# Eleven weight blocks multiplied in full precision, and a new order of gate work at the head of each chunk

## The chip, the cores and the metric

The kernel runs on one core of one Trainium2 chip. The metric is the device time of one execution in microseconds (us). A core has five engines that run side by side, each through its own list of instructions in order: TensorE (PE, matrix products; its weight loads are shown apart as PEld), VectorE (DVE), ScalarE (ACT), GpSimd (POOL) and SyncE (SP), which here only starts transfers. They wait for one another through semaphores.

## What is computed

One encoder block on 512 tokens of 1024 numbers. A first half (a convolution and a recurrence, projections in and out) makes `x1`; the second half, where this change lies, is a PEER layer: of 16384 one-neuron experts each token picks 16 per head, for 8 heads.

```
q = (h @ w_q);  sc = q . sub_keys                # two 128-wide score rows per head
top_s, top_i = top_k(sc, 16)                     # per half
best_s, best_pos = top_k(all 16 x 16 sums, 16)   # the 16 experts of a head
g = softmax(best_s)
act = gelu(expert_u[idx] . h)
y = sum_k g * act * expert_v[idx]
x = x + g2 * y;  out = rmsnorm(x)
```

## The kernel before, in words

The tokens stand in four tiles of 128. For the tokens from 192 on (320 of them, `NU`) the kernel doesn't gather experts: it multiplies every block of 128 experts with all of them and masks the result by gates. For tile 0 and the first 64 tokens of tile 1 it gathers rows of `expert_u` and `expert_v` by index: one gather on POOL and one product with a sum on DVE (a *dot step*, `scr`, L823) for each.

**Precision.** A product of two float32 operands is made of three products in the reduced format `fp32r`. ACT rounds a weight block to `whi` (`high`, L75), DVE subtracts it from the block to get the rest, `wlo` (`low`, L80), and PE multiplies `whi` by the rounded activations, `whi` by their rest and `wlo` by the rounded ones (`mm3`, L89, L90, L91): 8 slices of 128 rows times 3, so 24 products of 128x320 a block.

**Phases.** A first half; the queries and scores; then the *activation phase*: a loop over `k`, one *chunk* for each of 124 weight blocks of `expert_u` (`CE`), with PE results evicted by ACT through GELU (`u_evict`, L888, two PSUM buffers). Then the *output phase*, 128 blocks of `expert_v` (`acc`, L1070) with the last four of `expert_u` among them, and the sums for the gathered rows (`ys`, L839); last the final norm.

**The order in the activation phase** is written by a planner when the program is built. It keeps three accounts of nanoseconds by fixed costs, `pe`, `dve` and `ac`, and fills each chunk with items of DVE work until the `dve` account reaches the `pe` account. An engine then simply follows its list. The generators are:

- `s`, the searches: the top 16 of the scores and of the candidate sums of a tile (`topk_tile`). It ends in one-hot comparisons for which ACT spreads a key over 2048 numbers (`oh`, L604) and takes the exponent for the softmax (L607). The exponent and GELU each load their table first.
- `r`, the top 16 of the scores for the remaining tiles. When it has ended, the gates may begin.
- `g`, the gates. One item of the wide kind prepares 8 tokens: DVE makes one-hots (`oh`, L662) and their high halves times the gate (`igh`, L667); ACT makes the low halves, one instruction a token (`gates_low`, L678, also `igh`). The item also issues, on PE, the 16 products (L693) of the group prepared by the `g` item before it, and on ACT the copies (`stg`, L702) of the one before that, which are stored to memory in pieces of 512 KB (`Gd`). A narrow kind (L652, L655, L690) serves 4 tokens, with float32 products; there are 16 such steps.
- `d`, the dot steps.

In a chunk `k` the kernel starts the load of block `k+5`, issues `low` for block `k+2`, the 24 products and the eviction of the chunk before, up to four low halves; then come the items, and at the end `high` for block `k+3`. The three loads for blocks 2 to 4 stand ahead of the loop. `HEAD` lets DVE's account begin 6000 ns low, so that the first chunks take more items.

Of the kernel before, what the change touches and what calls it, by code (L numbers as in the profile page):

```python
# [8 lines left out]
F32 = mybir.dt.float32  # L9
FR = mybir.dt.float32r  # L10
# [3 lines left out]
AF = mybir.ActivationFunctionType  # L14
# [3 lines left out]
T = 512  # L18
D = 1024
KB = 8  # L20
# [14 lines left out]
def block_kernel(ctx, tc, xT, small, w_ada1, w_ada, b_ada, w_in, w_r, w_i, w_out, w_q, keys, uT, u, v, final_g, out):  # L35
    nc = tc.nc
# [4 lines left out]
    wring = ctx.enter_context(tc.tile_pool(name="wring", bufs=2))  # L41
# [26 lines left out]
    def load_w(src):  # L68
        raw = wring.tile([128, KB, 128], F32, name="wraw", bufs=WR)
        nc.sync.dma_start(raw, src)  # L70
        return raw
# [15 lines left out]
    def mm3(ps, hi, lo, xh, xl, ks, first, last):  # L87
        for k in ks:
            nc.tensor.matmul(ps, hi[:, k, :], xh(k), start=first and k == ks[0], stop=False)  # L89
            nc.tensor.matmul(ps, hi[:, k, :], xl(k), start=False, stop=False)  # L90
            nc.tensor.matmul(ps, lo[:, k, :], xh(k), start=False, stop=last and k == ks[-1])  # L91
# [12 lines left out]
    adac = const.tile([128, 48], F32, name="adac")  # L104
# [114 lines left out]
    def modulate(t1, k, A, B, hh, hl, full=None):  # L219
        f = sq_pool.tile([128, T], F32, name="mfull")  # L220
        nc.vector.tensor_scalar(f, t1, A[:, k:k + 1], B[:, k:k + 1], op0=OP.mult, op1=OP.add)
        nc.scalar.activation(hh[:, k, :], t1, AF.Identity, scale=A[:, k:k + 1], bias=B[:, k:k + 1])
        nc.vector.tensor_sub(hl[:, k, :], f, hh[:, k, :].bitcast(F32))
        if full is not None:
            full(k, f)
# [15 lines left out]
    z_, tn, e_, w_, w2, ac = (l4[:, i, :] for i in range(6))  # L241
# [166 lines left out]
    for m in range(KB):  # L408
# [3 lines left out]
        ps = psZ.tile([128, T], F32, name="ps_z", bufs=3)  # L412
# [31 lines left out]
    A2 = const.tile([128, KB], F32, name="A2")  # L444
    nc.vector.scalar_tensor_tensor(A2, adac[:, 32:40], 1.0, sm("n2g"), op0=OP.add, op1=OP.mult)
    h2n = persist.tile([128, D], F32, name="h2n")
    sel = ctx.enter_context(tc.tile_pool(name="sel", bufs=1, side="right"))
    h2b = sel.tile([128, D], F32, name="h2b")

    def full2(k, f):  # L450
        if k % 4 == 0:
# [10 lines left out]
    for k in range(KB):  # L462
        t1 = sq_pool.tile([128, T], F32, name="mt1")
        nc.vector.tensor_mul(t1, xs[:, k, :], psr2)
        modulate(t1, k, A2, adac[:, 24:32], h2h, h2l, full2)


    ep = ExitStack()
    ring = ctx.enter_context(tc.tile_pool(name="ring", bufs=1, side="right"))
    scp = ep.enter_context(tc.tile_pool(name="scp", bufs=1, side="right"))  # L470
    top = scp.tile([128, NT, 8, 2, 16], F32, name="top")
    ti = scp.tile([128, NT, 8, 2, 16], U32, name="ti")
# [25 lines left out]
    qsp = {}  # L498
    early = chain(*(stage1([h], range(NT)) for h in range(HQ)))

    ND = T - 128
    NU = ND - XB
    hd = lambda k: h2h[:, k, T - NU:]
    ld = lambda k: h2l[:, k, T - NU:]

    for h in range(8):
# [8 lines left out]
        ps = psZ.tile([128, T], F32, name="ps_z", bufs=3)  # L515
# [50 lines left out]
    def topk_tile(t):  # L566
# [17 lines left out]
        g = g_s.rearrange("p (h k) -> p h k", h=8) if t == 0 else topk.tile([128, 8, 16], F32, name="g")  # L584
# [12 lines left out]
        for w in range(2):  # L597
            oh = topk.tile(shp, F16, name="oh")
            if w == 1:
                pf = topk.tile([128, 8, 16], F16, name="pf")  # L600
                nc.vector.tensor_copy(pf, msk)
            yield None
            key, ref, cmp, src = ((pf, st16, OP.is_ge, dif), (pf, io16, OP.is_equal, tif[:, :, 1, :]))[w]
            nc.scalar.activation(oh, key[:, :, :, None].to_broadcast(shp), AF.Copy)  # L604
            ac[0] += 1930
            if w == 0:
                nc.scalar.activation(g, g, AF.Exp)  # L607
            yield None
            nc.vector.tensor_tensor(oh, oh, ref[:, None, None, :].to_broadcast(shp), op=cmp)
            nc.vector.tensor_tensor(oh, oh, src[:, :, None, :].to_broadcast(shp), op=OP.mult)  # L610
            yield 2300
            for n in (8, 4, 2):
                nc.vector.tensor_add(oh[:, :, :, 0:n], oh[:, :, :, 0:n], oh[:, :, :, n:2 * n])
            nc.vector.tensor_add(ij[:, w], oh[:, :, :, 0], oh[:, :, :, 1])
            yield 1400
# [57 lines left out]
    def gates_low(n):  # L673
        for _ in range(n):
            if lows:
                of, ig, gl, t0 = lows[0]
                k = next(low_k)
                nc.scalar.activation(ig[:, 1, k // 2, :, k % 2], of[:, k // 2, 0, :, k % 2], AF.Copy,  # L678
                                     scale=gl[:, t0 + k:t0 + k + 1])
                if k == 7:  # L680
                    lows.pop(0)
# [165 lines left out]
    jobs = [("u", c) for c in range(CE)]  # L847
# [4 lines left out]
    wraw, whi, wlo = {1: qraw[9]}, {}, {}  # L852
# [3 lines left out]
    def w_load(k):  # L856
        if k < len(jobs):
            kind, i = jobs[k]
            wraw[k] = load_w(uT[i] if kind == "u" else
                             v[vorder[i] * 128:(vorder[i] + 1) * 128, :].rearrange("p (k e) -> p k e", k=KB))  # L860

    def w_high(k):
        if k < len(jobs):
            whi[k] = high(wraw[k])

    def w_low(k):
        if k < len(jobs):
            wlo[k] = low(wraw.pop(k), whi[k])

    def weights(k):  # L870
# [3 lines left out]
    act = {0: act0}  # L874
# [15 lines left out]
    def u_chunk(k, pool):  # L890
        c = jobs[k][1]
        if c:
            ps = pool.tile([128, NU], F32, name="ps_act", bufs=2)
            mm3(ps, whi.pop(k), wlo.pop(k), hd, ld, range(KB), True, True)
            u_evict()
            unread.append((c, ps))
        q = c // 2 - RB // 2 + 2
        if c % 2 == 0 and 0 <= q < v0 // 2:
            spill(q)
        pe[0] += 3530  # L900
        dve[0] += 1140
        ac[0] += 1400

    gbuf, g16, gdone = {}, {}, set()
    coef = {}
# [71 lines left out]
    def turn(k):  # L977

        awake = [g for g in "gsrd" if g in gens and asleep[g] <= k]
        if "d" in awake and (given["d"] >= DR * (k + 1 - first[0]) or k >= CE - QU or xd > k % 2):  # L980
            awake.remove("d")
        if gopen and "g" in gens:
            gt = 96 * (k + 1 - gopen[0]) / (KD - KG - gopen[0])
            if "g" in awake and given["g"] < gt and ac[0] < pe[0] + AD:
                return "g"
            if "s" in awake and (given["g"] < gt or given["s"] < NS * (k - gopen[0]) / (SE * (KD - gopen[0]))):
                return "s"
        elif "s" in awake:
            return "s"
        elif "r" in awake and ("d" not in awake or given["d"] >= DS * (k - first[0])):  # L990
            return "r"
        for g in "dsg" if ac[0] < pe[0] + AD else "ds":
            if g in awake:
                return g
# [8 lines left out]
    for k in range(CE):  # L1003
        weights(k)
        u_chunk(k, psE)
        gates_low(4)
        cur[0] = k
        if sready and not first:
            first.append(k + 4)
            asleep["d"] = k + 4  # L1010
            for m in range(GB_E - 1):
                gath(u, usteps[m][0], usteps[m][3], m)
        ac[0] = max(ac[0], pe[0] - LEAD)
        dve[0] = max(dve[0], RHO * pe[0] - LEAD - (HEAD if k < 9 else 0))
        xd = 0
        while dve[0] < RHO * pe[0] or k == KD:
            g = turn(k)
            if k == KD:
                g = next((g for g in "sg" if g in gens), None)
                if "s" not in gens and len(bdone) < XB:  # L1020
                    g = "d"
            if g is None or (g == "d" and "g" not in gens and xd >= XD):
                break
            n = next(gens[g], 0)
            if n == 0:
                assert g != "d"
                late_k[g] = k
                del gens[g]
                continue
            if n is None:  # L1030
                asleep[g] = k + 1
                continue
            dve[0] += n
            xd += g == "d"
            if gopen or g == "d":
                given[g] += {"g": 0, "d": 1}.get(g, n)
        w_high(k + 3)
        if k == KD:
            ep.close()
            vp = ctx.enter_context(tc.tile_pool(name="vp", bufs=2, reuse_waits="tile"))  # L1040
            gp = ctx.enter_context(tc.tile_pool(name="gp", bufs=1, reuse_waits="tile"))
            late[:] = [gp, taken[0] + 10]
            gt8 = vp.tile([128, 2, NG, 8, 16], F32, name="gt", bufs=1)
        m = k - CE + XE
        if 0 <= m < XE:
            for n in [0] if m < 2 else range(5) if m == XE - 1 else [8]:
                v_gates(n)
        if m >= XE - 2:
            (v_gated, v_rest)[m - XE + 2](0)
# [105 lines left out]
XB = 64  # L1155
GS = 32768.0
GPE = 460
SE = 0.65
AD = 500
LEAD = 3500  # L1160
RHO = 1.0
VE = 1
KG = 4
HEAD = 6000
NS = 56000
DS = 1.0
XD = 2
# [60 lines left out]
```

## Time and profile before

| | |
|---|---|
| median of 3 runs | 1394.5 us (1393.42 to 1398.49) |
| profiled execution, whole | 1394.83 us |
| its span, first to last instruction | 1393.0 us |
| mean granted TensorE clock | 0.985 |
| activation phase, chunks 1 to 123 | 294 to 817 us of the span |
| output phase and end | 817 to 1393 us |

The span is what the trace covers; 1.8 us of the profiled execution lie around it. In the views that follow, a line such as `L80` is a line of the kernel before, "out<-in" names what an instruction writes and reads, and a bracket at the end of a row of the timeline is the idle time of that engine just before the instruction, with what ended it.

### The profile page before, as it was taken

The page shows a single profiled execution, that of the slowest core. Times are in us where ns is not written, and L with a number is a line of the kernel's source. Part 1 is how long each engine was busy: PE and PEld are TensorE (multiplying, and loading weights), DVE is VectorE, ACT ScalarE, POOL GpSimd, SP SyncE. Part 2 cuts the span into 40 slices and gives each one's busy share as a digit, 9 for nine tenths or more (in the row PEclk, how much of TensorE's full clock was granted, in tenths as well). Part 3 has the DMA queues.
Part 4 walks back from the last instruction along what each step waited for, and adds up shares of the span by engine and source line. Part 5 has one row for each costly group of instructions (what it writes and reads, how often), then busy time and mean ns, then how long its engine had stood idle before and what let it go on. Part 6 is the DMA issues. An engine that isn't in the chain of part 4 may idle for free.

```text
span 1393.0 us, 21402 instructions
## 1 busy us (share of the span) xinstructions
PE 1321.6 (95%) x7571; PEld 1135.5 (82%) x7571; DVE 1235.1 (89%) x2313; ACT 706.6 (51%) x1202; POOL 532.7 (38%) x334
## 2 busy tenths in 40 slices
PE   5999999989999999999999999899999999999995
PEld 2676787789989899998999998787878787878884
DVE  6878756999999999999999748799999889898998
ACT  4666644434567797787744443333243334333442
POOL 0000000000233244445445305576766566676760
PEclk9999999999999999999999999999999999999998
DMA  8776322224688899999999988999999999999994
GB/s 349 264 271 219 115 91 84 69 92 133 230 287 292 289 369 394 331 377 361 417 381 395 411 274 278 391 392 416 413 415 413 398 404 413 411 415 412 418 380 171
DMA packets 146928, 440.06 MB, mean 316 GB/s; under 512 B 14722, under 2 KB 42370, under 8 KB 144772
## 3 DMA queue, kind: packets, MB, share of 16 engines
q1 hardware_dynamic: 99812, 267.75, 52.2%
q0 software_dynamic: 46720, 169.89, 31.0%
q8 instruction: 59, 0.97, 0.3%
q10 hardware_dynamic: 288, 1.05, 0.2%
q14 instruction: 49, 0.40, 0.1%
HBM read 393.54 MB, written 45.09 MB: 315 GB/s over the span
## 4 chain that ended last, share of the span: by engine, by line
PE 47%; DVE 22%; DMA 13%; issue 12%; ACT 5%; DVEq 0%; SPq 0%; POOL 0%; ACTq 0%
DMA wraw<-in_v_dram 10%; PE acc L1070 8%; PE ps_act L89 6%; PE ps_act L91 6%; PE ps_act L90 6%; PE ps_z L89 5%; PE ps_z L90 5%; PE ps_z L91 5%; DVE wlo L80 4%; DVE scr L823 4%; DVE ys L839 3%; DMA Gd<-stg 2%; DVE cl L965 2%; DVE cf L954 2%; PE ps_gt L693 2%
## 5 line engine op out<-in xcount | busy, mean ns | idle before, releaser
L75 ACT ACTIVATE whi<-wraw 128x1024 fp32r<-128x1024 f32 x292 | 308.7, 1057 | 361.2 <-DMA wraw<-in_v_dram 204.6
L80 DVE TENSOR_TENSOR wlo<-wraw,whi 128x1024 fp32r<-128x1024 f32 x292 | 356.2, 1220 | 91.5 <-ACT whi L75 90.3
L89 PE MATMUL ps_act<-h,whi 128*128 128x320 f32 x1016 | 321.2, 316 | 5.4 <-ACT act L888 5.2
L91 PE MATMUL ps_act<-h,wlo 128*128 128x320 f32 x1016 | 316.2, 311 | 4.0 <-DVE wlo L80 4.0
L90 PE MATMUL ps_act<-h,whi 128*128 128x320 f32 x1016 | 315.9, 311 | 0.0
L802 POOL DMA_INDIRECT rows<-in_u_dram,idx_s x128 | 200.0, 1562 | 187.1 <-DVE scr L823 159.9
L802 POOL DMA_INDIRECT rows<-in_v_dram,idx_s x128 | 218.6, 1708 | 112.2 <-DVE ys L839 89.1
L1070 PE MATMUL acc<-whi,cl 128*128 128x512 f32 x750 | 233.5, 393 | 9.0 <-DVE cl L965 8.9
L1070 PE MATMUL acc<-whi,ch 128*128 128x512 f32 x750 | 232.8, 392 | 6.6 <-ACT ch L958 6.0
L1070 PE MATMUL acc<-wlo,ch 128*128 128x512 f32 x750 | 232.0, 390 | 0.0
L802 POOL DMA_INDIRECT rows<-in_u_dram,idx_b x64 | 108.9, 1702 | 264.4 <-DVE scr L823 171.6
L89 PEld LDWEIGHTS ps_act<-h,whi 128*128 128x128 f32 x1016 | 192.9, 190 | 8.0 <-ACT act L888 7.1
L91 PEld LDWEIGHTS ps_act<-h,wlo 128*128 128x128 f32 x1016 | 192.6, 190 | 4.3 <-DVE wlo L80 4.3
L90 PEld LDWEIGHTS ps_act<-h,whi 128*128 128x128 f32 x1016 | 192.8, 190 | 0.2
L1070 PEld LDWEIGHTS acc<-whi,cl 128*128 128x128 f32 x750 | 140.2, 188 | 43.5 <-DVE cl L965 15.1
L1070 PEld LDWEIGHTS acc<-whi,ch 128*128 128x128 f32 x750 | 140.7, 189 | 37.9 <-ACT ch L958 8.3
L1070 PEld LDWEIGHTS acc<-wlo,ch 128*128 128x128 f32 x750 | 141.4, 188 | 29.8
L839 DVE SCALAR_TENSOR_TENSOR ys<-rows,acts,ys 128x1024 f32<-128x1024 f32 x127 | 162.6, 1281 | 1.7
L823 DVE SCALAR_TENSOR_TENSOR scr<-rows,h2n 128x1024 f16<-128x1024 f32 x128 | 156.2, 1220 | 2.7 <-DMA rows<-in_u_dram,idx_s 1.0
L678 ACT ACTIVATE igh<-oh,gl 128x128 f16<-128x128 f16 x320 | 104.0, 431 | 47.3 <-DVE oh L662 47.1
L433 POOL DMA_DIRECT2D x1d<-xn x8 | 4.5, 570 | 258.8 <-ACT xn L432 258.8
L888 ACT ACTIVATE act<-ps_act 128x320 f32<-128x320 f32 x127 | 54.9, 433 | 90.6 <-PE ps_act L91 90.4
(277 smaller groups left out, 1750.6 us busy)
## 6 DMA issues: line engine op xcount, KB each, us to landing
wraw<-in_uT_dram SPq DMA_DIRECT2D x128, 512.0 KB, 6.4
wraw<-in_v_dram SPq DMA_DIRECT2D x128, 512.0 KB, 10.2
Gd<-stg SPq DMA_DIRECT2D x46, 512.0 KB, 8.9
wada<-in_w_ada_dram SPq DMA_DIRECT2D x16, 1024.0 KB, 5.3
Ad<-act SPq DMA_DIRECT2D x48, 320.0 KB, 7.0
act<-Ad SPq DMA_DIRECT2D x48, 320.0 KB, 12.6
h<-Gd SPq DMA_DIRECT2D x12, 1024.0 KB, 17.3
wraw<-in_w_in_dram SPq DMA_DIRECT2D x20, 512.0 KB, 6.0
```

The costliest lines, as they stand in the source:

```text
L75: nc.scalar.activation(hi, raw, AF.Copy)
L80: nc.vector.tensor_sub(lo, raw, hi.bitcast(F32))
L89: nc.tensor.matmul(ps, hi[:, k, :], xh(k), start=first and k == ks[0], stop=False)
L90: nc.tensor.matmul(ps, hi[:, k, :], xl(k), start=False, stop=False)
L91: nc.tensor.matmul(ps, lo[:, k, :], xh(k), start=False, stop=last and k == ks[-1])
L678: nc.scalar.activation(ig[:, 1, k // 2, :, k % 2], of[:, k // 2, 0, :, k % 2], AF.Copy, scale=gl[:, t0 + k:t0 + k + 1])
L693: nc.tensor.matmul(pg[:, k, :], oh[:, a, 1, :, b], ig[:, w, a, :, b], start=w == 0, stop=w == 1)
L802: nc.gpsimd.indirect_dma_start(out=r[:, :], out_offset=None, in_=table, in_offset=bass.IndirectOffsetOnAxis(ap=idxs[:, k:k + 1], axis=0))
L823: nc.vector.scalar_tensor_tensor(scr, rows.pop(n), 1.0, hn, op0=OP.mult, op1=OP.mult, accum_out=dst[:, k:k + 1])
L839: nc.vector.scalar_tensor_tensor(ys, rows.pop(k), acts[:, k:k + 1], ys, op0=OP.mult, op1=OP.add)
L888: nc.scalar.activation(act[c // 2][:, c % 2], ps, AF.Gelu)
L1070: nc.tensor.matmul(accs[b][e], st[:, bs], mv[:, e * 512:(e + 1) * 512], start=first, stop=last)
```

## The change

1. **Blocks 1 to 11 of `expert_u` unsplit.** For `k < FN = 12` there is neither `high` nor `low`. PE multiplies the raw float32 block by a float32 copy of the activations, `h2f`: 8 products in place of 24. The copy is made when the activations are: one more ACT instruction of 128x320 for each of 8 slices, in four buffers that the ring `act` otherwise uses later. Blocks 5 to 11 are loaded into the buffers of `whi` and `wlo`, which are free then.
2. **Accounts.** Such a chunk counts 4400 ns on `pe` (`FPE`), nothing for the subtraction on `dve` and 450 on `ac`. `HEAD` is 0.
3. **One `g` item a chunk.** After a `g` item the gates sleep until the next chunk. Dot steps may run ahead a little by the number of chunks since the gates ended (`DX`).
4. **ACT at the head of a chunk.** `high(k+3)` stands right behind the eviction, then up to 8 low halves instead of 4.
5. In the search of tile 1 one more pause of a chunk ahead of the first one-hots.

```
+    h2f = [ring.tile([128, 2, NU], F32, name="act", bufs=RB // 2) for _ in range(KB // 2)]
...
         modulate(t1, k, A2, adac[:, 24:32], h2h, h2l, full2)
+        nc.scalar.activation(h2f[k // 2][:, k % 2], t1[:, T - NU:], AF.Identity, scale=A2[:, k:k + 1],
+                             bias=adac[:, 24 + k:25 + k])
...
             yield None
+            if t == 1 and w == 0:
+                yield None
...
     def w_load(k):
+            if 5 <= k < FN:
+                raw = wring.tile([128, KB, 128], FR, name=("wlo", "whi")[k % 2], bufs=WB).bitcast(F32)
+                nc.sync.dma_start(raw, uT[i])
+                wraw[k] = raw
+                return
     def w_high(k):
-        if k < len(jobs):
+        if FN <= k < len(jobs):
     def w_low(k):
-        if k < len(jobs):
+        if FN <= k < len(jobs):
...
     def u_chunk(k, pool):
-            mm3(ps, whi.pop(k), wlo.pop(k), hd, ld, range(KB), True, True)
+            if k < FN:
+                raw = wraw.pop(k)
+                for j in range(KB):
+                    nc.tensor.matmul(ps, raw[:, j, :], h2f[j // 2][:, j % 2], start=j == 0, stop=j == KB - 1)
+            else:
+                mm3(ps, whi.pop(k), wlo.pop(k), hd, ld, range(KB), True, True)
...
-        pe[0] += 3530
-        dve[0] += 1140
-        ac[0] += 1400
+        pe[0] += FPE if c and k < FN else 3530
+        dve[0] += 0 if c and k < FN - 2 else 1140
+        ac[0] += 450 if c and k < FN - 3 else 1400
...
-        if "d" in awake and (given["d"] >= DR * (k + 1 - first[0]) or k >= CE - QU or xd > k % 2):
+        if "d" in awake and (given["d"] >= DR * (k + 1 - first[0]) + DX * max(k - late_k.get("g", k), 0) or k >= CE - QU or xd > k % 2):
...
         weights(k)
         u_chunk(k, psE)
-        gates_low(4)
+        w_high(k + 3)
+        gates_low(8)
...
+            if g == "g" and k < KD:
+                asleep[g] = k + 1
...
-        w_high(k + 3)
...
+FN = 12
+DX = 0.3
+FPE = 4400
-HEAD = 6000
+HEAD = 0
```

On PE the first chunks read as follows. Before, the start of chunk 1 (`h_83` are the activations in the reduced format):

```order
L89 MATMUL ps_act<-h_83,whi 128x320
L90 MATMUL ps_act<-h_83,whi 128x320
L91 MATMUL ps_act<-h_83,wlo 128x320
L89 MATMUL ps_act<-h_83,whi 128x320
L90 MATMUL ps_act<-h_83,whi 128x320
L91 MATMUL ps_act<-h_83,wlo 128x320
```

Now, chunks 1 to 9 (32 products for chunks 1 to 4, whose blocks lie in `wraw`, then 8 a chunk; the `act` that is read is `h2f`):

```order
L907 MATMUL ps_act<-act,wraw 128x320 x32
L907 MATMUL ps_act<-act,whi 128x320 x8
L907 MATMUL ps_act<-act,wlo 128x320 x8
L907 MATMUL ps_act<-act,whi 128x320 x8
L907 MATMUL ps_act<-act,wlo 128x320 x8
L907 MATMUL ps_act<-act,whi 128x320 x8
```

No product of chunks 1 to 11 waits for ACT or DVE any more, apart from the eviction of its buffer.

On DVE, the chunk that holds the sixth and seventh wide group (chunk 28), before:

```order
L80 TENSOR_TENSOR wlo<-wraw,whi 128x1024
L662 TENSOR_TENSOR oh_4095<-io_2603,selT 128x2048
L667 TENSOR_TENSOR igh<-oh_4095,gh 128x1024
L823 SCALAR_TENSOR_TENSOR scr,act_b<-rows,h2b 128x1024
L662 TENSOR_TENSOR oh_4133<-io_2603,selT 128x2048
L667 TENSOR_TENSOR igh<-oh_4133,gh 128x1024
L80 TENSOR_TENSOR wlo<-wraw,whi 128x1024
```

Now, the seventh and eighth wide group (chunks 26 and 27):

```order
L80 TENSOR_TENSOR wlo<-wraw,whi 128x1024
L667 TENSOR_TENSOR oh_3869<-io_2615,selT 128x2048
L672 TENSOR_TENSOR igh<-oh_3869,gh 128x1024
L828 SCALAR_TENSOR_TENSOR scr,act_b<-rows,h2b 128x1024
L80 TENSOR_TENSOR wlo<-wraw,whi 128x1024
L828 SCALAR_TENSOR_TENSOR scr,act_b<-rows,h2b 128x1024
L604 CAST pf<-msk 128x128
L667 TENSOR_TENSOR oh_3948<-io_2615,selT 128x2048
L672 TENSOR_TENSOR igh<-oh_3948,gh 128x1024
```

Two groups no longer stand in one chunk. Before, the second `g` item of such a chunk had PE multiply the group that the first one had only just prepared; chunks 28, 39 and 82 held two wide groups, and chunks 94, 98, 102, 106 and 110 two narrow ones.

On ACT, the same chunk 28 before, with the eviction of chunk 28 at its end (`high` is the last piece of a chunk):

```order
L888 ACTIVATE act<-ps_act 128x320
L678 ACTIVATE igh<-oh_3968,gl 128x128 x4
L702 ACTIVATE stg<-ps_gt 128x128x4 x2
L678 ACTIVATE igh<-oh_4095,gl 128x128 x8
L702 ACTIVATE stg<-ps_gt 128x128x4 x2
L75 ACTIVATE whi<-wraw 128x1024
L888 ACTIVATE act<-ps_act 128x320
```

And now, in chunks 26 to 28:

```order
L898 ACTIVATE act<-ps_act 128x320
L75 ACTIVATE whi<-wraw 128x1024
L707 ACTIVATE stg<-ps_gt 128x128x4 x2
L898 ACTIVATE act<-ps_act 128x320
L75 ACTIVATE whi<-wraw 128x1024
L683 ACTIVATE igh<-oh_3869,gl 128x128 x8
L707 ACTIVATE stg<-ps_gt 128x128x4 x2
L898 ACTIVATE act<-ps_act 128x320
```

The rounding has moved from behind the low halves and copies to ahead of them, and all 8 low halves of a group stand in the chunk after the one in which DVE prepared it.

More of the change, by code (lines that the diff above doesn't have):

```diff
@@ L448, in block_kernel @@
     h2b = sel.tile([128, D], F32, name="h2b")
+    ring = ctx.enter_context(tc.tile_pool(name="ring", bufs=1, side="right"))
+    ND = T - 128
+    NU = ND - XB
+    h2f = [ring.tile([128, 2, NU], F32, name="act", bufs=RB // 2) for _ in range(KB // 2)]
     def full2(k, f):
@@ L465, in block_kernel @@
         modulate(t1, k, A2, adac[:, 24:32], h2h, h2l, full2)
+        nc.scalar.activation(h2f[k // 2][:, k % 2], t1[:, T - NU:], AF.Identity, scale=A2[:, k:k + 1],
+                             bias=adac[:, 24 + k:25 + k])
     ep = ExitStack()
-    ring = ctx.enter_context(tc.tile_pool(name="ring", bufs=1, side="right"))
     scp = ep.enter_context(tc.tile_pool(name="scp", bufs=1, side="right"))
@@ L499, in block_kernel @@
     early = chain(*(stage1([h], range(NT)) for h in range(HQ)))
-    ND = T - 128
-    NU = ND - XB
     hd = lambda k: h2h[:, k, T - NU:]
```

## The prediction

> **What bounds the kernel now.** I read the page's busy shares first, then the stages, then who waited for whom on PE and DVE, and last the rows around PE's long waits.
>
> ```profile
> PE 1321.6 (95%) x7571; PEld 1135.5 (82%) x7571; DVE 1235.1 (89%) x2313; ACT 706.6 (51%) x1202; POOL 532.7 (38%) x334
> core 0: us, PE busy (x) PEld busy (x) DVE busy (x) ACT busy (x) POOL busy (x), PEclk, DMA share, GB/s
> 294.00:342.50 48.50, 42.52 (x272) 41.40 (x268) 47.72 (x225) 23.35 (x30) 0.00 (x0) 0.93 0.37 114
> 342.50:412.00 69.50, 65.87 (x489) 64.43 (x489) 69.04 (x261) 38.31 (x85) 20.80 (x13) 1.00 0.70 235
> 412.00:465.00 53.00, 48.30 (x349) 46.80 (x350) 47.93 (x84) 37.28 (x75) 17.96 (x11) 0.97 0.90 316
> 465.00:640.00 175.00, 172.77 (x1387) 169.54 (x1385) 172.62 (x339) 146.59 (x326) 71.59 (x41) 1.00 0.94 347
> 640.00:690.00 50.00, 47.35 (x368) 46.50 (x369) 48.70 (x63) 39.48 (x96) 27.78 (x19) 0.93 1.02 410
> 690.00:750.00 60.00, 56.73 (x409) 55.91 (x408) 54.47 (x106) 25.81 (x45) 28.53 (x20) 1.00 1.02 386
> 750.00:817.00 67.00, 66.81 (x469) 66.55 (x467) 49.97 (x79) 29.33 (x45) 21.65 (x16) 1.00 1.03 388
> 817.00:1360.00 543.00, 527.65 (x2325) 432.67 (x2326) 490.99 (x536) 201.36 (x259) 339.23 (x203) 0.99 1.00 392
> ```
>
> In the activation phase (294 to 817) both PE and DVE are nearly full up to 690; from 750 DVE has room. So the phase is worth what PE loses in it, as long as DVE can follow. PE loses most in 294 to 342, 412 to 465 and 640 to 690, which are also the stages where the granted clock (PEclk) is below 1. These are its waits from 294 to 817, and DVE's from 285 to 700 (us in total, times, longest):
>
> ```profile
> PE ps_gt L693 <- DVE igh L667: 6.5, 2, 3.3
> PE ps_act L89 <- ACT act L888: 5.2, 5, 1.6
> PE ps_act L91 <- DVE wlo L80: 4.0, 1, 4.0
> PE ps_gt L690 <- DVE oh L655: 2.3, 1, 2.3
> PE ps_gt L693 <- ACT igh L678: 1.9, 2, 1.3
> PE ps_gt L690 <- ACT stg L702: 0.9, 1, 0.9
> DVE wlo L80 <- ACT whi L75: 8.1, 6, 3.0
> DVE st L554 <- PE ps_g L525: 1.7, 1, 1.7
> ```
>
> DVE waits 9.8 us in 415: it is the second bound, right behind PE.
>
> **The change part by part.**
>
> *Float32 products.* Now, 24 products of a block take the distance of these two rows, 3.52 us; eleven blocks 38.7. The two rows of float32 products in the trace follow.
>
> ```profile
> 294.60 0.31 PE L89 MATMUL ps_act<-h,whi 128*128 128x320 f32 x1
> 298.12 0.31 PE L89 MATMUL ps_act<-h,whi 128*128 128x320 f32 x1
> 48.81 1.04 PE L135 MATMUL ps_row<-wada,cs 128*1 128x512 f32 x8
> L135 PE MATMUL ps_row<-wada,cs 128*1 128x512 f32 x128 | 16.6, 591 | 0.0
> 750.66 1.78 PE ps_gt L690 x16
> L690 PEld LDWEIGHTS ps_gt<-oh x128: 186/192/192, 697.2 to 774.2; 128*128 128x128 f32 x128
> ```
>
> L690 is issued 64 times and recorded 128 times: a float32 product is two records. At L135 four products, each one output row, run side by side; eight records last 1.04 us, one lasts 0.591, so the second four start about 0.43 after the first four, and 320 columns would take 0.27 a record. At L690 16 records of 128 columns follow each other in 1.78 us, 0.111 each; in proportion 320 columns take 0.278. A block is 16 records: 4.3 or 4.45 us. I take 4.35, nearer the wider row. The low end is one record at the reduced format's pace, 16 times 0.147 or 2.35. Eleven blocks: +9.1 us (-12.9 to +10.2).
>
> *What the first eleven chunks lose now.* The stage 294 to 342.5 holds them: 48.5 less 38.7, so 9.8 us are lost. The largest part is the wait of chunk 3 for its `wlo`, and what comes behind it:
>
> ```profile
> 305.69 0.64 PE L91 MATMUL ps_act<-h,wlo 128*128 128x320 f32 x1 [4.04 <-DVE wlo L80]
> 306.12 0.47 PE L89 MATMUL ps_act<-h,whi 128*128 128x320 f32 x1
> 306.39 0.47 PE L90 MATMUL ps_act<-h,whi 128*128 128x320 f32 x1
> ```
>
> Products follow at 0.27 instead of 0.147 after it: the granted clock is low for some us. Unsplit blocks wait for neither `whi` nor `wlo`; their loads find free buffers (DMA share 0.37). So -9.8, and chunk 12 starts about when it did (+9.1 - 9.8). Their evictions stay, hidden on an ACT half idle.
>
> *DVE and ACT gain.* Eleven subtractions and roundings go:
>
> ```profile
> L75 ACT ACTIVATE whi<-wraw 128x1024 fp32r<-128x1024 f32 x292 | 308.7, 1057 | 361.2 <-DMA wraw<-in_v_dram 204.6
> 285.00:342.50 57.50, 15.81 (x13) 0.94 0.38 119
> 342.50:700.00 357.50, 103.00 (x85) 0.99 0.90 331
> L888 ACT ACTIVATE act<-ps_act 128x320 f32<-128x320 f32 x127 | 54.9, 433 | 90.6 <-PE ps_act L91 90.4
> ```
>
> The middle two rows are `wlo` alone on DVE: 15.81/13 is 1.216 us each, so 13.4 us, or 12.9 with the overlap of neighbours (1.13 to 1.22 apart). DVE enters chunk 12 that much further ahead in its list. `HEAD` at 0 takes items out of the first chunks, where no product waits for DVE now: no cost. The pause in tile 1's search is a chunk in which DVE has other items: none either.
>
> *One group a chunk.* The three chunks with two wide groups cost PE these waits:
>
> ```profile
> 413.66 2.12 PE L693 MATMUL ps_gt<-igh,oh 128*128 128x128 f16 x16 [3.22 <-DVE igh L667]
> 460.50 0.60 PE L693 MATMUL ps_gt<-igh,oh 128*128 128x128 f16 x7 [1.33 <-ACT igh L678]
> 642.65 2.12 PE L693 MATMUL ps_gt<-igh,oh 128*128 128x128 f16 x16 [3.29 <-DVE igh L667]
> 644.52 0.61 PE L89 MATMUL ps_act<-h,whi 128*128 128x320 f32 x1
> 644.93 0.47 PE L90 MATMUL ps_act<-h,whi 128*128 128x320 f32 x1
> ```
>
> That is 7.8 us. The clock of the two stages adds (1 - 0.97) x 53 + (1 - 0.93) x 50 = 5.1. Together -12.9, and the waits go because the products now read a group from an earlier chunk. By the Trainium skill (TensorE: Matmul & The Clock Gate, Part 1) the clock drops only after about 3.4 us of idling; the trace disagrees, since 3.22 and 3.29 are followed by records 0.41 and more apart, so I keep the 5.1. By the rule the item would be -7.8 and the sum 5.1 smaller.
>
> The next two rows, a low half on ACT and one of PE's waits for an eviction, go with the items behind them.
>
> ```profile
> L678 ACT ACTIVATE igh<-oh,gl 128x128 f16<-128x128 f16 x320 | 104.0, 431 | 47.3 <-DVE oh L662 47.1
> 351.23 0.41 PE L89 MATMUL ps_act<-h,whi 128*128 128x320 f32 x1 [1.47 <-ACT act L888]
> ```
>
> *High at the head, eight low halves.* Four of DVE's six waits for `whi` (8.1 us) end in chunks with two groups, where rounding stands behind low halves and copies; they shrink. Price: a search with its exponent blocks ACT, and evictions behind it made PE wait 5.2 us in five places. Two of these lie before 352, where the search of tile 1 stood beside split blocks; three stay, and four more low halves ahead of each (104.0/320, so 0.33 apart) can add 1.3: between 0 and +3.9, taken as +1, since PE has a second buffer.
>
> *The rest.* From 342.5 to 412 PE idles 3.6 us, of it 1.5 behind tile 1's exponent (the last row): -2. The narrow pairs: -1.5 of the 2.3 and 0.9, because the second stands behind this wait for a store, which stays:
>
> ```profile
> 705.35 0.60 ACT L702 ACTIVATE stg<-ps_gt 128x512 f32<-128x512 f32 x1 [6.99 <-DMA Gd<-stg]
> ```
>
> The copy `h2f` is eight ACT instructions of 128x320 (0.43 us by L888) between 224 and 245 us. There PE follows at once and `mt1` has two buffers; hidden it costs 0, exposed 3.5. I take +0.5: in that stretch ACT mostly waits.
>
> *The sum.* PE: 9.1 - 9.8 - 12.9 + 1 - 2 = -14.6 up to 690. DVE allows 12.9, and up to 8.1 more if all its waits for `whi` go. I put PE one us short of its own sum, -13.6, for chunks with groups in a row where DVE is only a chunk ahead. Behind 690: -1.5; the copy: +0.5. Together -14.6. The output phase has the same transfers, products and sums (113 dot steps in the chunks before it instead of 112), so it moves as a whole. The span goes from 1393.0 to 1378.4; with the 1.8 us around it 1380.2, against 1394.83 for the profiled run, which stands 0.3 above the median. I say 1380.
>
> **The rivals.**
>
> *DVE keeps the bound.* The 13 us that DVE saves are filled at once with other items, since the planner fills every chunk up to PE's account; DVE arrives at the pair chunks as late as before, and the waits there become waits for `wlo` or `igh` in other chunks. Then only 9.8 + 2 + 1.5 stand against 9.1 + 1.5: -2.7, 1392. For it: DVE is at 172.62 of 175 in the long stage. Against it: the items total the same and the subtractions are gone, so DVE must end them earlier.
>
> *The output phase takes it back.* Its DMA share is 1.00 and 392 GB/s; if its end hangs on bytes and the transfers don't start earlier, the time stays 1394. Against it: the mean holds a slack start.
>
> ```profile
> 817.00:870.00 53.00, 52.66 (x266) 45.96 (x267) 37.46 (x47) 21.68 (x29) 19.72 (x13) 1.00 0.76 262
> ```
>
> *Slower: float32 weight loads exposed.* A load lasts 0.192. If PE can't hide it behind a float32 product, a block costs 16 x 0.19 = 3.0 more, eleven 33: 1413. It decides from 5.7 us a block on (4.35 + 14.6/11). Against it: at L690 records with such loads are 0.111 apart. By the Trainium skill (TensorE: Matmul & The Clock Gate, Part 3, "What overlaps and what doesn't") loads overlap only with products in other rows of the array, which speaks for this rival; the trace disagrees at L690.
>
> **How the numbers follow.** A half per cent, 7 us, is what a measurement can tell here. The forecast has 0.68, with a range of its own of 1371 (all of DVE's waits gone as well) to 1387 (the exponent waits at their dear end, the copy exposed). DVE keeping the bound: 0.18 (1388 to 1394). The output phase: 0.06 (1394). Exposed loads: 0.05. The remaining 0.03 lies on both sides. So faster 0.69, same 0.24, slower 0.07. From 1371 to 1394 about 0.86 is held; the upper end can't come down without losing the second case.
>
> **What would show it.** Float32 records 0.27 apart and 4.35 us from chunk to chunk; chunk 12 at about 342; no wait over 2 us on `igh` or `wlo`; PEclk 1.00 in all slices from 294 to 817; the output phase at about 802, 576 us long as before. Wrong I am if DVE's `wlo` becomes PE's main wait after 342, if ACT's evictions cost more than 6 us, or if the output phase grows by what the other gains.

## Result and the profile after

| | before | after |
|---|---|---|
| median, 6 runs each | 1396.01 us (1393.42 to 1398.49) | 1382.45 us (1381.26 to 1384.01) |
| span of the profiled execution | 1393.0 | 1381.1 |
| its mean granted clock | 0.985 | 0.990 |
| chunk 12 starts / output phase starts | 342.5 / 817.3 | 340.9 / 808.75 |

The ratio is 0.9905, with a 95% interval of 0.9892 to 0.9918: faster by 13.6 us, close to the 1380 forecast. The way there was only partly the one foreseen. First the busy shares and the stages of the changed kernel, with the columns of before:

```profile
PE 1325.2 (96%) x7483; PEld 1126.6 (82%) x7483; DVE 1222.7 (89%) x2302; ACT 700.7 (51%) x1199; POOL 528.9 (38%) x334
core 0: us, PE busy (x) PEld busy (x) DVE busy (x) ACT busy (x) POOL busy (x), PEclk, DMA share, GB/s
294.00:342.50 48.50, 48.50 (x186) 34.57 (x185) 48.05 (x295) 15.69 (x22) 0.00 (x0) 1.00 0.22 68
342.50:412.00 69.50, 64.42 (x475) 61.95 (x474) 68.70 (x196) 47.80 (x107) 23.23 (x15) 0.98 0.74 257
412.00:465.00 53.00, 53.00 (x419) 52.38 (x419) 52.42 (x130) 39.87 (x92) 18.42 (x12) 1.00 0.91 318
465.00:640.00 175.00, 172.51 (x1374) 168.24 (x1373) 171.62 (x297) 143.39 (x316) 76.22 (x46) 1.00 0.98 369
640.00:690.00 50.00, 48.02 (x368) 47.03 (x366) 48.51 (x75) 35.17 (x81) 25.30 (x17) 0.97 1.03 417
690.00:750.00 60.00, 60.00 (x437) 60.00 (x436) 55.87 (x110) 25.98 (x41) 16.99 (x16) 1.00 1.00 376
```

PE is busy in all of 294 to 342.5, 412 to 465 and 690 to 750. What it still waits for (294 to 806), and what DVE waits for (285 to 700), in total, times, longest:

```profile
PE ps_act L89 <- ACT act L898: 5.6, 3, 2.3
PE ps_t L779 <- ACT g L777: 2.0, 1, 2.0
PE ps_act L91 <- DVE wlo L80: 0.8, 1, 0.8
PE ps_t L633 <- DVE g L624: 0.7, 1, 0.7
PE ps_gt L698 <- DVE igh L672: 0.3, 1, 0.3
DVE st L557 <- PE ps_g L528: 4.2, 1, 4.2
DVE oh L657 <- PE ps_gt L695: 1.1, 3, 0.4
DVE gl L642 <- ACT gh L640: 1.1, 1, 1.1
DVE wlo L80 <- ACT whi L75: 1.0, 1, 1.0
```

The waits for groups of one-hots (`igh`) are gone but for 0.3 us. PE's listed waits sum to 9.4 us, against 22.1 before; DVE's for `whi` fell from 8.1 to 1.0. DVE's first row is a wait that ends as chunk 1 begins, and was 1.7 before. The unsplit products, shown by the tile they read:

```profile
L907 PE MATMUL ps_act<-act,wraw x64: 432/432/537, 293.7 to 310.8; 128*128 128x320 f32 x64
```

and the first split product behind the eleven blocks, from the timeline:

```profile
340.94 0.55 PE L89 MATMUL ps_act<-h,whi 128*128 128x320 f32 x1
```

The 64 records of four blocks start from 293.7 to 310.8, so 17.1/63 = 0.27 apart. From chunk 1 (293.7) to chunk 12 (340.9) eleven blocks take 47.2 us, 4.29 each.

### The profile page after: what moved, and what is told of

It reads as the page before. It is cut to its first block, busy times and chain, and to the rows that moved or that the text cites. A ratio compares the mean times of both kernels' runs of the same rounds, so it can differ in the third digit from the quotient of the medians.

```text
span 1381.1 us, 21224 instructions
## 1 busy us (share of the span) xinstructions
PE 1325.2 (96%) x7483; PEld 1126.6 (82%) x7483; DVE 1222.7 (89%) x2302; ACT 700.7 (51%) x1199; POOL 528.9 (38%) x334
## 4 chain that ended last, share of the span: by engine, by line
DVE 32%; PE 21%; issue 21%; DMA 18%; ACT 4%; POOL 2%; DVEq 0%; SPq 0%; POOLq 0%; ACTq 0%
DMA wraw<-in_v_dram 14%; DVE wlo L80 7%; DVE scr L828 6%; PE ps_z L89 5%; PE ps_z L90 5%; PE ps_z L91 5%; DVE ys L844 3%; DMA wraw<-in_uT_dram 2%; DVE oh L667 2%; POOL rows L807 2%; DVE cf L969 2%; DVE cl L980 2%; ACT whi L75 1%; ACT igh L683 1%; PE ps_row L135 1%
## 5 line engine op out<-in xcount | busy, mean ns | idle before, releaser
L75 ACT ACTIVATE whi<-wraw 128x1024 fp32r<-128x1024 f32 x281 | 297.1, 1057 | 357.7 <-DMA wraw<-in_v_dram 192.8
L80 DVE TENSOR_TENSOR wlo<-wraw,whi 128x1024 fp32r<-128x1024 f32 x281 | 342.9, 1220 | 84.3 <-ACT whi L75 83.3
L89 PE MATMUL ps_act<-h,whi 128*128 128x320 f32 x928 | 293.8, 317 | 5.6 <-ACT act L898 5.6
L91 PE MATMUL ps_act<-h,wlo 128*128 128x320 f32 x928 | 288.1, 310 | 0.8 <-DVE wlo L80 0.8
L90 PE MATMUL ps_act<-h,whi 128*128 128x320 f32 x928 | 288.0, 310 | 0.0
L807 POOL DMA_INDIRECT rows<-in_u_dram,idx_s x128 | 192.5, 1504 | 213.6 <-DVE scr L828 183.4
L807 POOL DMA_INDIRECT rows<-in_v_dram,idx_s x128 | 225.5, 1762 | 107.4 <-DVE ys L844 82.5
L807 POOL DMA_INDIRECT rows<-in_u_dram,idx_b x64 | 105.7, 1651 | 235.0 <-DVE scr L828 112.2
L89 PEld LDWEIGHTS ps_act<-h,whi 128*128 128x128 f32 x928 | 175.6, 189 | 7.8 <-ACT act L898 6.6
L91 PEld LDWEIGHTS ps_act<-h,wlo 128*128 128x128 f32 x928 | 175.4, 189 | 1.0 <-DVE wlo L80 1.0
L90 PEld LDWEIGHTS ps_act<-h,whi 128*128 128x128 f32 x928 | 175.6, 189 | 0.2
L1087 PEld LDWEIGHTS acc<-whi,cl 128*128 128x128 f32 x750 | 140.3, 188 | 39.5 <-DVE cl L980 10.8
L898 ACT ACTIVATE act<-ps_act 128x320 f32<-128x320 f32 x127 | 54.9, 432 | 139.5 <-PE ps_act L91 101.6
L683 ACT ACTIVATE igh<-oh,gl 128x128 f16<-128x128 f16 x320 | 99.7, 432 | 20.7 <-DVE oh L667 20.5
```

The lines of the kernel that those rows point to most:

```text
L75: nc.scalar.activation(hi, raw, AF.Copy)
L80: nc.vector.tensor_sub(lo, raw, hi.bitcast(F32))
L807: nc.gpsimd.indirect_dma_start(out=r[:, :], out_offset=None, in_=table, in_offset=bass.IndirectOffsetOnAxis(ap=idxs[:, k:k + 1], axis=0))
L898: nc.scalar.activation(act[c // 2][:, c % 2], ps, AF.Gelu)
L1087: nc.tensor.matmul(accs[b][e], st[:, bs], mv[:, e * 512:(e + 1) * 512], start=first, stop=last)
```

## The experiments

The theory was the prediction's: the unsplit blocks take away the wait of chunk 3, one group a chunk takes away those for `igh`, and DVE's saved 13 us let it follow. The rivals: another part of the change (`HEAD`, the order on ACT) brings the gain; or the remaining waits for ACT decide the time. For each run the table has PE's listed waits (294 to 805), DVE's for `whi` (285 to 700), the start of the output phase, and the median with its ratio to the kernel before, run beside it on the same chip (its medians there: 1396.25, 1396.38 and 1395.77).

| kernel | PE waits | DVE for `whi` | output starts | median | ratio (95%) |
|---|---|---|---|---|---|
| before | 22.1 | 8.1 | 817.3 | 1396.01 | |
| after | 9.4 | 1.0 | 808.8 | 1382.45 | 0.9905 (0.9892 to 0.9918) |
| only_unsplit | 13.4 | 7.3 | 814.4 | 1392.58 | 0.9973 (0.9960 to 0.9986) |
| only_order | 19.8 | 6.5 | 815.8 | 1391.03 | 0.9964 (0.9948 to 0.9980) |
| head0 | 14.1 | 8.8 | 809.8 | 1390.20 | 0.9956 (0.9939 to 0.9972) |
| high_end | 13.9 | 9.6 | 815.1 | 1390.15 | 0.9958 (0.9941 to 0.9974) |
| low_first | 12.0 | 6.1 | 810.4 | 1389.18 | 0.9953 (0.9935 to 0.9970) |
| act_old | 10.0 | 4.9 | 808.8 | 1385.08 | 0.9921 (0.9901 to 0.9941) |
| low4 | 9.9 | 1.3 | 807.0 | 1381.11 | 0.9892 (0.9866 to 0.9917) |
| two_groups | 10.1 | 2.6 | 810.2 | 1385.97 | 0.9923 (0.9907 to 0.9939) |
| no_exp | 5.3 | 1.1 | 806.5 | 1381.82 | 0.9885 (0.9863 to 0.9908) |
| exp_later_mm | 8.3 | 0.2 | 804.3 | 1384.58 | 0.9918 (0.9900 to 0.9936) |
| fn24 | 3.8 | 3.2 | 803.9 | 1383.18 | 0.9914 (0.9893 to 0.9935) |
| all_later | 0.9 | 3.0 | 804.8 | 1380.95 | 0.9894 (0.9872 to 0.9917) |

The waits and the start of the output phase come from one profiled execution of each kernel, the median from all of its runs. The profiled execution was the slowest of its kernel for `only_order` (1396.99), `head0` (1394.24), `two_groups` (1388.74) and `no_exp` (1382.20), and the fastest for `low_first` (1385.92), `act_old` (1384.12), `fn24` (1381.14) and `exp_later_mm` (1380.50). So a few us between a stage of a profile and a median tell nothing.

**The two halves of the change.** `only_unsplit` keeps the unsplit blocks, their accounts and `HEAD` at 0, without points 3 to 5 of the change:

```
-            if g == "g" and k < KD:
-                asleep[g] = k + 1
-        w_high(k + 3)            # at the head
-        gates_low(8)
+        gates_low(4)
+        w_high(k + 3)            # at the chunk's end
-            if t == 1 and w == 0:
-                yield None
-DX = 0.3
+DX = 0.0
```

> The unsplit blocks 1 to 11 and their accounts alone (with HEAD at 0); gates, rounding and low halves in the order of before. Theory 1 (PE's long waits lie in chunks with two wide groups, and the order removes them, while DVE's saved subtractions only give it room): the first eleven chunks end at about 341 as in the changed kernel (342.5 before, so -1.5), but chunks with two wide groups are still there with waits of 2 to 3 us and a half clock behind them; 1386 to 1394. Theory 2 (DVE is the bound, and the 13 us of subtractions are the gain): as fast as the changed kernel, 1380 to 1385.

`only_order` keeps points 3 to 5 and splits every block (the copy `h2f` is dropped too):

```
-FN = 12
-HEAD = 0
+FN = 1
+HEAD = 6000
```

> One group a chunk, rounding and low halves at the chunk's head, the pause and the dot steps' allowance alone; all blocks split, HEAD at 6000 as before. Theory 1: the waits of the pair chunks (7.8 us and a slow clock worth 5) go, but DVE waited only 9.8 us before and can't give more than that: 1386 to 1391, with new waits of PE for wlo or igh. Theory 2 (only DVE's saved work counts): no change, 1393 to 1398. Rival 3 (the order alone is the gain, the float32 blocks cost what they save): 1380 to 1385.

They brought 3.7 and 5.2 us, less together than the 13.6 of the whole. The waits of each, PE's and DVE's:

```profile
PE ps_act L89 <- ACT act L896: 6.3, 3, 3.8
PE ps_gt L696 <- ACT igh L681: 3.4, 1, 3.4
DVE wlo L80 <- ACT whi L75: 7.3, 7, 3.0
```

```profile
PE ps_gt L696 <- ACT igh L681: 6.7, 1, 6.7
PE ps_act L91 <- DVE wlo L80: 4.6, 2, 4.0
PE ps_act L89 <- ACT act L896: 3.5, 3, 2.3
```

Without the new order DVE still waits 7.3 us for `whi`; without unsplit blocks and with `HEAD` as before the 4.0 us wait for `wlo` stays. Each half leaves waits standing that the whole change doesn't have. In `only_order` that includes 6.5 us of DVE's waits for `whi`, all between 640 and 700, although the rounding stands at the head.

**HEAD alone.** `head0` is the kernel before with one number changed; every block is split.

```
-HEAD = 6000
+HEAD = 0
```

> The kernel before with HEAD at 0 and nothing else. Theory 1 (the first chunks' wait of 4.0 us and the slow clock behind it come from the extra items, but DVE is full up to 690 and must do them later): the wait goes, chunk 12 starts at 336 to 340, and it comes back as waits for wlo or igh up to 690: 1392 to 1398. Rival (the account alone made the first stretch's gain, unsplit blocks were not needed for it): 1385 to 1390.

This run overturned the theory's first step. Its window of 294 to 342.5:

```profile
294.00:342.50 48.50, 47.16 (x328) 46.41 (x327) 46.80 (x232) 26.74 (x34) 0.00 (x0) 1.00 0.42 131
```

The 4 us wait is gone, the clock is 1.00, PE gets 328 records through instead of 272, and chunk 12 starts at 334.4, 6.5 us sooner than in the changed kernel, since split blocks cost 3.52 and not 4.29. The wait of chunk 3 came from the extra items that `HEAD` put ahead of `wlo` on DVE. The gain is 5.6 us, not less than that of `only_unsplit`. The two kernels differ only in the unsplit blocks with their accounts and copy, so in the old order these bring nothing that shows (+2.4 us, with overlapping intervals). Split blocks with `HEAD` at 0 and points 3 to 5 were not run, so what the unsplit blocks bring in the new order stays open; if the gains simply added, `head0` and `only_order` would make 10.8 of the 13.6 us without one unsplit block. In the profiled execution of `head0` the output phase starts at 809.8, only 1.0 later than in the changed kernel, and then lasts 582.6 us, the longest of all; how the 5.6 us of the medians divide between the phases is not known.

**The order on ACT.** Four kernels from the changed one: `high_end` moves `w_high(k + 3)` back to the chunk's end and keeps eight low halves at the head; `low_first` swaps the two at the head; `act_old` does as before (four at the head, rounding at the end); `low4` only goes back to four low halves.

```
         w_high(k + 3)      # high_end, act_old: at the end;  low_first: behind the next line
         gates_low(8)       # act_old, low4: gates_low(4)
```

> The changed kernel with the rounding of block k+3 at the end of the chunk's items again; low halves stay at the head. Theory 1 (rounding behind low halves and copies made DVE wait 8.1 us for whi before, and 3 to 6 us of that would return): 1384 to 1389, with DVE waits for whi of 3 us or more in all between 342 and 690. Rival (with one group a chunk ACT is early enough anyway): 1381 to 1384.

> The changed kernel with the two pieces at a chunk's head exchanged: eviction, up to eight low halves, then the rounding of block k+3. Theory 1 (what hurt with the rounding at the chunk's end was that copies, spread keys and table loads stood ahead of it; at the head, behind 2.6 us of low halves, it is still early): 1381 to 1385. Rival (rounding must stand ahead of the low halves, since DVE waits for whi and then PE for its evictions): 1387 to 1391, as with rounding at the end (1390).

> The changed kernel with ACT's order of before: four low halves at the head of a chunk and the rounding at its end; unsplit blocks and one group a chunk stay. Theory 1 (eight low halves and rounding at the end work against each other; with four the rounding at the end costs less): 1385 to 1389, between the changed kernel and the 1390 of rounding at the end with eight. Rival (ACT's order is worth nothing by itself): 1381 to 1384. Second rival (one group a chunk brings nothing without the new order on ACT): 1391 to 1394, as the unsplit blocks alone (1392.6).

> The changed kernel with up to four low halves at the head of a chunk instead of eight. Theory 1 (eight low halves ahead of an exponent make its wait longer, four take 1.3 us out of the way): PE's waits of 2.3 us for evictions shrink to about 1 us, and chunks with groups in a row wait up to 1.3 us more for low halves, three times: 1380 to 1384. Rival (the number of low halves at the head is what makes the change fast): 1386 or more.

Against the changed kernel `high_end` is 7.7 us slower, `low_first` 6.7, `act_old` 2.6 (with overlapping intervals), and `low4` the same (-1.3). For `low_first` the rival held: rounding has to stand ahead of the eight low halves. Waits of `high_end`, then of `low_first`:

```profile
PE ps_act L89 <- ACT act L898: 10.3, 7, 3.2
DVE wlo L80 <- ACT whi L75: 9.6, 8, 2.3
```

```profile
PE ps_act L89 <- ACT act L898: 9.0, 5, 3.3
DVE wlo L80 <- ACT whi L75: 6.1, 5, 2.3
```

Eight low halves are 2.5 us on ACT. With rounding behind them `whi` comes late, DVE waits 5 to 9 us more, and DVE has little to spare up to 690 (in the changed kernel it is busy for 341 of the 347.5 us from 342.5 on). Rounding ahead of eight low halves is the largest single piece that was isolated inside the changed kernel. With four low halves the place of the rounding is worth less (`act_old` to `low4`: 4.0 us, with overlapping intervals).

**One group a chunk.**

```
-            if g == "g" and k < KD:
-                asleep[g] = k + 1
```

> The changed kernel without the rule of one group a chunk; all else as changed. Theory 1 (a second group in a chunk makes PE multiply what DVE and ACT have only just made, at 1.3 to 3.4 us a time and a slow clock behind it): three or more such waits come back, 1387 to 1392. Rival (with DVE 13 us ahead the second group is ready, the rule is not what counts): 1380 to 1384.

Undone, it costs 3.5 us (with overlapping intervals), and one wait of the old kind is back, where three or more were expected:

```profile
PE ps_gt L698 <- DVE igh L672: 3.8, 1, 3.8
```

That is much less than the 12.9 booked for this step; the other parts remove most of those waits too.

**The waits that are left.** `no_exp` replaces the softmax's exponent by a copy, so that no table is loaded for it; its gates are not the softmax. `exp_later_mm` keeps the exponent, moves it behind the sums of the first one-hots, a chunk or two later, and puts a chunk between the GELU of L777 and the product that reads it (L779). `fn24` leaves 23 blocks unsplit; `all_later` is both.

```
-                nc.scalar.activation(g, g, AF.Exp)       # no_exp
+                nc.scalar.activation(g, g, AF.Copy)
...
                 nc.vector.tensor_copy(pf, msk)
+                nc.scalar.activation(g, g, AF.Exp)       # exp_later_mm, all_later
...
-            if w == 0:                                   # exp_later_mm, all_later
-                nc.scalar.activation(g, g, AF.Exp)
...
             nc.scalar.activation(act_p[es, es], act_b[es, :], AF.Gelu)
+        yield None                                       # exp_later_mm, all_later
...
-FN = 12
+FN = 24                                                  # fn24, all_later
```

> The changed kernel with the softmax's exponent replaced by a copy, so that ACT loads no table in the activation phase; the gates' values are therefore not the softmax. Theory 1 (PE's three waits for an eviction, 5.6 us and two dips of the clock, come from the two table loads of 1.28 us behind eight low halves): these waits go, 4 to 7 us less than the changed kernel, 1375 to 1379. Rival: DVE has only 2 to 4 us of lead in the middle of the phase, so half of it comes back as waits for wlo: 1379 to 1382.

> The changed kernel with the exponent of the softmax issued a chunk or two later, away from the spreading of the key (1.9 us on ACT in the same chunk), and with one chunk between the last GELU on ACT for the gates of tile 1 and the PE product that reads it (PE waits 2.0 us there). Theory 1 (these ACT blocks make PE wait 2.3, 2.3 and 2.0 us, with a slow clock behind each): 3 to 6 us less than the changed kernel, 1376 to 1380. Rival (DVE is full up to 690 and takes most of it back, as when the table loads were left out, where the output phase began 2.2 us earlier): 1380 to 1383.

> The changed kernel with blocks 1 to 23 unsplit instead of 1 to 11. A float32 block costs PE 0.77 us more than a split one in the changed kernel's trace (4.29 against 3.52) and saves DVE 1.17. Theory 1 (PE and DVE are both nearly full up to 690, so a float32 block helps only as far as it takes waits out): 12 blocks add 9.2 us to PE and can take at most the waits left between 342 and 690, some 10 us with the dips of the clock, away: 1381 to 1390. Rival (DVE is the bound, every subtraction saved is time saved): 1368 to 1376.

> The changed kernel with 23 unsplit blocks, the exponent a chunk or two later and one chunk between the last GELU for the gates and its product: the three that started the output phase earliest (803.9 and 804.3, against 808.8). Theory 1 (what each of them takes off PE in the activation phase adds up, as long as DVE has room, which 23 unsplit blocks give it): output phase from 797 to 802 and 1374 to 1380. Rival (the output phase gives it back, being 572 to 577 long whenever it starts earlier): 1380 to 1384 with the phase starting at 800 or before.

None is told apart from the changed kernel: 1381 to 1385 us, with overlapping intervals, and none clearly beats it. The gains that were expected of `no_exp`, `exp_later_mm` and `all_later` (1374 to 1380) didn't come. In `no_exp` the waits behind L898 fell from 5.6 to 1.4 us and PE's sum from 9.4 to 5.3; the output phase starts 2.3 sooner and the median is 0.6 lower. The stretch from 342.5 to 690, in the changed kernel, in `fn24` and in `all_later`:

```profile
342.50:690.00 347.50, 337.95 (x2629) 329.60 (x2628) 341.25 (x695) 266.23 (x593) 143.17 (x89) 0.99 0.93 346
```

```profile
342.50:690.00 347.50, 344.16 (x2570) 324.89 (x2569) 332.54 (x696) 261.43 (x588) 128.56 (x90) 1.00 0.94 352
```

```profile
342.50:690.00 347.50, 346.89 (x2568) 325.87 (x2567) 332.45 (x696) 261.31 (x588) 127.56 (x90) 1.00 0.94 351
```

In `fn24` twelve more unsplit blocks put 12 x 0.77 = 9.2 us more work on PE, and the time stays. DVE's busy time in the stretch falls from 341.25 to 332.54, and PE, waiting 5.6 us less, fills up instead. In `all_later` PE is busy for 346.89 of 347.5 and its listed waits are 0.9 us, yet the output phase starts only 4.0 us sooner and the median is 1.5 lower. By the busy times, DVE's bound has been traded for PE's.

## Why the prediction came out

- **The float32 block**: 4.35 a block forecast, 4.29 measured (+8.5 for +9.1). In part that is luck: at L135, 1.04 less 0.591 is 0.45 and not 0.43, which gives 4.5 a block. The loads are hidden, so the rival of exposed loads fell.
- **The first eleven chunks, -9.8**: the size was right (chunk 12 at 340.9, about 342 forecast), the cause was not. The step "Unsplit blocks wait for neither `whi` nor `wlo`" is true and doesn't decide. It was `HEAD` that made DVE late, and "`HEAD` at 0 ... no cost" was booked as nothing where it is a gain: `head0` alone takes the stall away. An edit worth 5.6 us by itself got a sentence.
- **One group a chunk, -12.9**: the waits went, but undoing this part alone gives back 3.5. The -12.9 belongs to several parts together, and 5.1 of it is clock, which hangs on more than the length of the waits (last section). "0.41 and more apart" holds for the first two records behind those waits only; the next stand 0.26 to 0.27 apart.
- **DVE keeps the bound**, a rival: not here, since DVE's wait for `whi` fell to 1.0. Its 1392 is the time of `only_unsplit` (1392.58), where DVE still waits 7.3 us for `whi`. That the saved subtractions pay once `whi` comes in time is not shown, since the new order with split blocks and `HEAD` at 0 wasn't run. And not all of the 12.9 us was a lead: 2.5 went into DVE's wait ahead of chunk 1 (L557, 4.2 against 1.7).
- **The output phase takes it back**, a rival: not here, that part got 3.3 us shorter.
- **High at the head, +1**: mis-sized, and the benefit was underrated. PE's waits for evictions cost 5.6 us in three places; before it was 5.2 in five, of which three were to stay at 1 us more. Two of the three, 2.3 us each, lie behind an exponent; the third (0.9, at 355.10) stands in `no_exp` too. The low halves and rounding ahead of the GELU of L777 made a wait that was not foreseen, 2.0 us. The gain from early rounding, put only as "they shrink", is 7.7 us with eight low halves. The rows on ACT ahead of that GELU, and PE's behind it:

```profile
670.58 2.48 ACT L683 ACTIVATE igh<-oh,gl 128x128 f16<-128x128 f16 x8
672.92 0.41 ACT L898 ACTIVATE act<-ps_act 128x320 f32<-128x320 f32 x1
673.24 1.04 ACT L75 ACTIVATE whi<-wraw 128x1024 fp32r<-128x1024 f32 x1
674.19 0.51 ACT L777 ACTIVATE g<-act_b 64x64 f32<-64x64 f32 x2
674.75 0.43 PE L779 MATMUL ps_t<-sel,g 128*128 128x64 f32 x2 [1.96 <-ACT g L777]
```

- **The rest, -2 and -1.5**: the wait of 1.5 us at 351.23 was put down to tile 1's exponent, wrongly. ACT loaded no table between 322 and 420 then; ahead of that eviction it stood still for 6.1 us, until DVE had written `gl`:

```profile
349.52 0.28 ACT L640 ACTIVATE selB<-ps_t 128x128 f32<-128x128 f32 x1 [6.14 <-DVE gl L637]
```

  The same instruction waits 7.55 us in the changed kernel and leaves PE the 0.9 us at 355.10. From 342.5 to 412 PE idles 5.1 us instead of 3.6, so the -2 didn't come. Of the narrow pairs' waits all 3.2 us went, not 1.5. The copy `h2f` cost nothing that shows: chunk 1 starts at 293.7, before at 294.6.
- **The chain of one exponent wait**, on ACT, then PE's row behind it:

```profile
390.57 2.49 ACT L683 ACTIVATE igh<-oh,gl 128x128 f16<-128x128 f16 x8 [2.18 <-DVE oh L667]
392.93 1.89 ACT L609 ACTIVATE oh<-pf 128x2048 f16<-128x2048 f16 x1
394.84 1.28 ACT L612 ACT_TABLE_LOAD   x1
396.13 0.31 ACT L612 ACTIVATE g<-g 128x128 f32<-128x128 f32 x1
396.35 1.07 ACT L707 ACTIVATE stg<-ps_gt 128x512 f32<-128x512 f32 x2
397.44 1.28 ACT L898 ACT_TABLE_LOAD   x1
398.73 0.44 ACT L898 ACTIVATE act<-ps_act 128x320 f32<-128x320 f32 x1
399.22 0.64 PE L89 MATMUL ps_act<-h,whi 128*128 128x320 f32 x1 [2.32 <-ACT act L898]
```

  From 390.57 on ACT works without a gap for 8.6 us, more than two chunks of 3.52, and the two PSUM buffers can't bridge that.
- **The sum**: -14.6 forecast in the span, -11.9 measured. Up to the output phase it was -8.6, of it -0.9 ahead of chunk 1 and -7.7 behind. For the -7.7: listed waits -12.7, clock -5.6 (8.5 us lost by (1 - PEclk) times the length of the stages before, 2.9 after), float32 +8.5; that makes -9.8, and 2.1 stay unexplained. The remaining -3.3 lies in the output phase and end (575.7 to 572.4), where 0 was forecast. In the profiled executions of these kernels that part lasts 572.4 to 582.6, so a few us there, and of any span, can't be put down to an edit.
- **PEclk 1.00 from 294 to 817**: not so, 0.98 and 0.97 in two stages.

## What to carry to other kernels

When a planner's constants are changed together with a visible edit, run each constant alone: here one number took away the stall that the edit seemed to remove. Where two engines are both nearly full, a wait removed from one shows up only until the other binds; look at the second engine's waits too (here DVE's for `whi`). `no_exp` took 4.1 us off PE's listed waits and left the time as it was; `high_end` put 8.6 us on DVE's waits for `whi` and 4.5 on PE's, and cost 7.7. On an engine that serves several others in order, put the short instruction with a waiting consumer ahead of the long batch.

## What the runs showed of the hardware

The granted clock does not follow from the length of a wait alone. In the changed kernel PE waited 2.32 us ahead of 399.22, 2.31 ahead of 584.36 and 1.96 ahead of 674.75. The windows behind the three, in order:

```profile
399.20:404.00 4.80, 4.78 (x23) 4.78 (x24) 4.77 (x6) 4.52 (x11) 1.80 (x2) 0.67 1.01 352
584.00:589.00 5.00, 4.64 (x41) 4.54 (x42) 4.93 (x6) 5.00 (x13) 0.89 (x1) 1.00 1.02 378
674.70:679.00 4.30, 4.25 (x19) 4.26 (x20) 4.27 (x9) 2.47 (x4) 2.34 (x2) 0.60 1.03 415
```

The first and third lost a third or more of the clock, with products 0.27 apart for about 3 us; the second lost none. In `high_end` an even longer wait was followed by full speed, 0.15 apart:

```profile
399.44 0.41 PE L89 MATMUL ps_act<-h,whi 128*128 128x320 f32 x1 [3.25 <-ACT act L898]
399.69 0.31 PE L90 MATMUL ps_act<-h,whi 128*128 128x320 f32 x1
399.84 0.30 PE L91 MATMUL ps_act<-h,wlo 128*128 128x320 f32 x1
```

So the length of a wait of 2 to 3.3 us doesn't decide whether a slow clock follows. Where the wait falls may decide it, but no run tested that; a term for it taken from one execution, like the 5.1 above, is no constant. The Trainium skill (TensorE: Matmul & The Clock Gate, Part 1) describes a free-running window of about 3.4 us over which activity is judged; a window that runs by itself would let a wait's position matter, which the rows above allow; that a drop needs about 3.4 us of idling doesn't fit them (1.96 sufficed).
